# Wider value projection, other accumulator banks and more raw weight tiles in a hybrid attention block

## The chip, the cores and the metric

The kernel runs on one core of one Trainium2 chip. The metric is the device time of one execution in microseconds (us); lower is better. Before the change three runs gave 1017.72, 1018.07 and 1017.91 us, with a median of 1017.91 us. About 0.2% of that, 2 us, is what counts here as a difference.

## The reference

The kernel computes one layer of an encoder block for 512 positions and 1024 channels, in float32. Cut to what matters:

```python
h = x + 0.5 * rms_norm(swiglu_1(rms_norm(x)))
u = rms_norm(h)
q_a, k_a, v_a, q_b, k_b, v_b = split(u @ w_in)          # 6 x 512 columns, heads of 64
o_a = stick_breaking_attention(q_a, k_a, v_a)           # 8 heads, strictly causal
o_b = chunk_band_attention(q_b, k_b, v_b, rel_bias)     # 8 heads, own chunk and the 8 before
h = h + rms_norm(concat(rms_norm(o_a), rms_norm(o_b)) @ w_out)
h = h + 0.5 * rms_norm(swiglu_2(rms_norm(h)))
h = h + rms_norm((p @ w_ple) * sigmoid(h @ w_gate))
```

The change touches the first matrix products of `swiglu_1`, the last ones of it, the query and key product of heads 0 to 3 of the first group, and `v_a`, the values of the first group's eight heads.

## The kernel before, in words

**Operands.** Activations lie transposed: `h` holds 1024 channels as eight blocks k of 128 partitions by 512 positions. Every float32 operand is split in two float32r parts, a rounded `hi` and the rest `lo`, and every product is three matmuls (`mm3`, L235: hi by hi, lo by hi, hi by lo), so lines L236 to L238 of the profile hold nearly all of TensorE's work.

**Weights.** They arrive in chunks of 128 partitions by 1024 columns (512 KB). Each chunk is read by a DMA into a raw tile, then split (`split_to`, L305): ScalarE casts it to `wh` (L307) and VectorE subtracts that from the raw tile to give `wl` (L308). Raw tiles have tags: `wr` with two buffers, `wx` with three, `wy` with one. A DMA into a tag waits until the chunk that held the buffer has been split. The SyncE queue issues the DMAs in order, so one that waits for a buffer holds back those behind it. The first feed-forward part begins with eight plain chunks (wgu, numbers 0 to 7), all on `wr`; from chunk 8 on come the chunks of a fast matrix scheme that also uses `wx` and `wy`.

**Start.** A loop over j loads the eight blocks of `x` (L734, L737), the first chunks (L736) and the identity (L748). The first four products (`f_pl`, one per 128 output columns) go through k = 0 to 7, twelve matmuls for each k. The squares of `x` are summed block by block into `acc` (ScalarE squares into one buffer, L302; VectorE adds, L303). After 25 products TensorE needs this sum: `n_ss`, L250, eight small matmuls.

**End of the first feed-forward part and the joint.** `tail` computes the last six output blocks in two halves of 256 positions (tiles `f_dt`); VectorE adds each to `f` (L636) and to the sum of squares. The joint computes queries and keys of the first four heads (`pj`, four accumulators) for each half while the normalisation of that half is still being applied by VectorE (L358, L359, L311).

**Mixer.** The values of the first group follow (`values`, L840): for i = 0 (heads 0 to 3) and i = 1 (heads 4 to 7), for each block tb of 128 positions, eight products of 256 columns, then an evacuation by ScalarE and VectorE (L853, L854). A work list (`PLAN`) hands such products out: `fill(n)` runs n steps of it between the attention's own matmuls. After 15 steps the scores of head 0 begin: `scores` (L859) gives tile `z`, ScalarE makes two sigmoids of it (`fa`, L877, and `be`, L878), GpSimd masks them, VectorE scans (L883) and multiplies (L884), TensorE transposes (`pt`, L914).

**Accumulators.** PSUM has four tags, A, B, z and T, of two banks each. A new tile takes a bank of its tag and waits until the tile that held it has been read.

**Order.** TensorE's order is the order of the code. The other engines' order is made by a scheduler at build time; on the chip each engine runs its own list strictly in order.

Of the kernel before, what the change touches and what calls it, by code (L numbers as in the profile page):

```python
# [16 lines left out]
P = 128  # L17
# [34 lines left out]
TAIL_ROOT = 3  # L52
PLAN = (("v", 0, 0), ("v", 0, 1), ("qk", 2), ("qk", 3), ("v", 1, 0), ("qk", 4), ("qk", 5), ("qk", 6), ("v", 1, 1), ("qk", 7))

@with_exitstack
def block_kernel(ctx, tc, xT, pT, gains, ident_d, bias_d, wgu1, wst1, wd1, wdst1, wqk, wv, wo, wgu2, wst2, wd2, wdst2, wpp, wpg, gple, out):
    nc = tc.nc
# [68 lines left out]
    qk_chunks = [(wqk[g, i, j], 1024) for g in range(2) for i in range(4) for j in range(2)]  # L128
    v_chunks = [(wv[g, i, c], 1024) for g in range(2) for i in range(2) for c in range(2)]
    chunks.extend(qk_chunks[:4])  # L130
    for kind, *at in PLAN:
        if kind == "qk":
            chunks.extend(qk_chunks[2 * at[0]:2 * at[0] + 2])
        else:
            chunks.extend(v_chunks[4 * at[0] + 2 * at[1]:4 * at[0] + 2 * at[1] + 2])
    out_chunks = [(wo[g, c], 1024) for g in range(2) for c in range(4)]
# [19 lines left out]
    def emit_dma(cuts=1, queues=(nc.sync,)):  # L156
# [3 lines left out]
        if isinstance(n, tuple):  # L160
# [242 lines left out]
    def ffn(name, u, sp, pl, go, gpre, sa, sb, fa):  # L403
# [327 lines left out]
    for j in range(4):  # L731
# [36 lines left out]
    with tc.tile_pool(name="mx", bufs=1, reuse_waits="tile") as mp:  # L768
# [55 lines left out]
        def project(s):  # L824
            g, i = divmod(s, 4)
            pss = []
            for j in range(2):
# [10 lines left out]
                yield  # L838

        def values(g, i, tag):  # L840
            t = mp.tile([P, 4, 4, 2, 64], F32R, name=f"v{g}{i}", tag="v", bufs=3)
            vt[g, i] = t
            w = [get(), get()]
            for tb in range(4):
                pv = psum(tag, f"pv{g}{i}_{tb}", HT)
                for k in range(KD):
                    hi, lo = w[k // 4]
                    q = slice((k % 4) * HT, (k % 4 + 1) * HT)
                    mm3(pv[:], um[0][:, k, tb * P:(tb + 1) * P], um[1][:, k, tb * P:(tb + 1) * P],
                        hi[:, q], lo[:, q], k == 0, k == KD - 1)  # L850
                    if k == KD - 1:
                        src = pv.rearrange("p (h d) -> p h d", d=64)
                        act.activation(t[:, tb, :, 0, :], src, AF.Copy, scale=Rc[:, tb:tb + 1])  # L853
                        dve.scalar_tensor_tensor(t[:, tb, :, 1, :], src, Rc[:, tb:tb + 1],  # L854
                                                 t[:, tb, :, 0, :].bitcast(F32), ALU.mult, ALU.subtract)
                    if k % 2:
                        yield
# [160 lines left out]
        def work_list():  # L1018
            for n, (kind, *at) in enumerate(PLAN):
                yield from project(*at) if kind == "qk" else values(*at, "A" if n else "B")  # L1020
            mix_f.append(big("fm", 1, F32))
# [138 lines left out]

_ARGS = ["xT", "pT", "gains", "ident", "bias", "wgu1", "wst1", "wd1", "wdst1", "wqk", "wv", "wo", "wgu2", "wst2", "wd2", "wdst2", "wpp", "wpg", "gple"]

# [32 lines left out]
def _layout(i):  # L1195
# [10 lines left out]
    w_in = np.asarray(i["w_in"])[0]  # L1206
    qk, v = [], []
    for g in range(2):
        w = w_in[:, 1536 * g:1536 * g + 1024].reshape(KD, P, 2, 4, P)
        qk.append(w.transpose(3, 2, 1, 0, 4).reshape(4, 2, P, KD * P))  # L1210
        w = w_in[:, 1536 * g + 1024:1536 * (g + 1)].reshape(2, 4, P, 2, HT)
        v.append(w.transpose(3, 0, 2, 1, 4).reshape(2, 2, P, 4 * HT))
    a["wqk"] = np.stack(qk)
    a["wv"] = np.stack(v)
    w = np.asarray(i["w_out"])[0].reshape(2, 4, P, 4, 2, P)
# [25 lines left out]
```

## Time and profile before

| what | value |
|---|---|
| three runs, median | 1017.91 us |
| the profiled execution | 1017.77 us |
| its span | 1016.1 us |
| TensorE busy | 1001.5 us, 99% |
| weight loads busy | 944.4 us, 93% |
| VectorE, ScalarE, GpSimd busy | 780.8, 590.7, 133.7 us |
| granted TensorE clock | 0.998 |
| HBM read | 134.31 MB |

The span runs from the first to the last instruction on the core; the execution's own time is 1.7 us longer. A row of the timeline has the start, the duration, engine, line, operation, tile written and tiles read, and in brackets how long the engine was idle before and what ended that. Durations of matmuls overlap, so what a matmul costs is the distance from its start to the next start.

### The profile page before, as it was taken

Reading aid. Unit: us, or ns where it says so; the run is one execution under the profiler, and the core shown is the slowest. Engines: PE = TensorE matmul, PEld = TensorE weight load, DVE = VectorE, ACT = ScalarE, POOL = GpSimd, SP = SyncE. Lnnn points to the kernel's source line nnn. Section 1 sums busy time; section 2 is a strip of 40 time slices with the busy share of each in tenths; the row PEclk is TensorE's granted clock in tenths of the full one; section 3 lists DMA queues with packets and bytes.
Section 4 is the critical chain, followed back from the end, with each engine's and each line's share of the span. In section 5 each row is a group of like instructions: output and inputs, shape, how many; then the busy total and the mean of one; then the engine's idle time right before and its main releaser. Section 6 shows DMA issues by size and latency. Waiting matters only on the chain.

```text
span 1016.1 us, 18477 instructions
## 1 busy us (share of the span) xinstructions
PE 1001.5 (99%) x7242; PEld 944.4 (93%) x7242; DVE 780.8 (77%) x1370; ACT 590.7 (58%) x993; POOL 133.7 (13%) x221
## 2 busy tenths in 40 slices
PE   9999999999999999999999999999999999999997
PEld 7889999999999999888898799899999999999886
DVE  6777777677667888999999868786777677666856
ACT  6456554454456466777889655565543563455553
POOL 0001112112220003344000000011122112210000
PEclk9999999999999999999999999999999999999999
DMA  7338888979885213313323302268788888875102
GB/s 276 103 102 186 162 173 192 202 168 183 195 190 176 105 38 110 94 53 105 113 84 94 119 28 63 52 142 190 168 181 194 181 169 203 178 191 184 55 12 84
DMA packets 44855, 139.71 MB, mean 137 GB/s; under 512 B 5216, under 2 KB 5600, under 8 KB 44768
## 3 DMA queue, kind: packets, MB, share of 16 engines
q0 software_dynamic: 14976, 50.34, 30.6%
q1 hardware_dynamic: 28368, 85.83, 24.7%
q10 hardware_dynamic: 1424, 2.36, 0.9%
q8 instruction: 57, 0.93, 0.4%
q14 instruction: 30, 0.25, 0.1%
HBM read 134.31 MB, written 2.10 MB: 134 GB/s over the span
## 4 chain that ended last, share of the span: by engine, by line
PE 90%; DVE 5%; ACT 2%; DMA 1%; issue 1%; SPq 0%; POOL 0%; DVEq 0%; ACTq 0%; POOLq 0%
PE f_a L238 9%; PE f_a L236 9%; PE f_a L237 9%; PE f_c L236 4%; PE f_c L237 4%; PE f_c L238 4%; PE pj L236 3%; PE pj L237 3%; PE pj L238 3%; PE f_b L236 2%; PE f_b L237 2%; PE f_b L238 2%; PE f_d L238 2%; PE f_d L236 2%; PE f_d L237 2%; PE pt L914 2%
## 5 line engine op out<-in xcount | busy, mean ns | idle before, releaser
L308 DVE TENSOR_TENSOR wl<-wx,wh 128x1024 fp32r<-128x1024 f32 (+1 forms) x104 | 118.4, 1140 | 39.5 <-ACT wh L307 38.5
L307 ACT CAST wh<-wx 128x1024 fp32r<-128x1024 f32 (+1 forms) x104 | 101.6, 983 | 66.9 <-DMA wx<-in_wst_dram 38.9
L308 DVE TENSOR_TENSOR wl<-wr,wh 128x1024 fp32r<-128x1024 f32 (+2 forms) x100 | 109.4, 1100 | 27.2 <-ACT wh L307 26.1
L307 ACT CAST wh<-wr 128x1024 fp32r<-128x1024 f32 (+2 forms) x100 | 94.3, 950 | 43.2 <-DMA wr<-in_wgu_dram 11.1
L211 POOL DMA_DIRECT2D wx<-in_wst_dram x54 | 47.0, 870 | 413.3 <-DVE wl L308 349.7
L307 ACT CAST wh<-wy 128x1024 fp32r<-128x1024 f32 (+1 forms) x52 | 51.2, 985 | 41.8 <-DMA wy<-in_wdst_dram 15.7
L308 DVE TENSOR_TENSOR wl<-wy,wh 128x1024 fp32r<-128x1024 f32 (+1 forms) x52 | 59.2, 1139 | 11.0 <-ACT wh L307 10.8
L236 PE MATMUL pj<-um_hi,wh 128*128 128x512 f32 (+1 forms) x160 | 56.9, 355 | 1.1 <-DVE f_f L636 1.1
L237 PE MATMUL pj<-um_lo,wh 128*128 128x512 f32 (+1 forms) x160 | 55.9, 349 | 0.3 <-DVE um_lo L311 0.3
L238 PE MATMUL pj<-um_hi,wl 128*128 128x512 f32 (+1 forms) x160 | 55.8, 349 | 0.0
L238 PE MATMUL f_a<-f_U6h,wl 128*128 128x256 f32 x144 | 40.6, 282 | 0.0
L238 PE MATMUL f_a<-f_U3h,wl 128*128 128x256 f32 x144 | 40.5, 282 | 0.0
L237 PE MATMUL f_a<-f_U6l,wh 128*128 128x256 f32 x144 | 40.5, 282 | 0.0
L236 PE MATMUL f_b<-f_U1h,wh 128*128 128x256 f32 x144 | 40.5, 282 | 0.0
L237 PE MATMUL f_b<-f_U1l,wh 128*128 128x256 f32 x144 | 40.5, 282 | 0.0
L236 PE MATMUL f_c<-f_U4h,wh 128*128 128x256 f32 x144 | 40.5, 282 | 0.0
L237 PE MATMUL f_a<-f_U0l,wh 128*128 128x256 f32 x144 | 40.5, 281 | 0.0
L237 PE MATMUL f_a<-f_U5l,wh 128*128 128x256 f32 x144 | 40.5, 281 | 0.0
L236 PE MATMUL f_a<-f_U0h,wh 128*128 128x256 f32 x144 | 40.5, 281 | 0.0
L236 PE MATMUL f_a<-f_U5h,wh 128*128 128x256 f32 x144 | 40.5, 281 | 0.0
L236 PE MATMUL f_c<-f_U2h,wh 128*128 128x256 f32 x144 | 40.5, 281 | 0.0
L236 PE MATMUL f_a<-f_U6h,wh 128*128 128x256 f32 x144 | 40.5, 281 | 0.0
(476 smaller groups left out, 3883.5 us busy)
## 6 DMA issues: line engine op xcount, KB each, us to landing
wx<-in_wst_dram POOLq DMA_DIRECT2D x54, 512.0 KB, 5.6
wx<-in_wst_dram SPq DMA_DIRECT2D x18, 512.0 KB, 4.6
wy<-in_wst_dram SPq DMA_DIRECT2D x18, 512.0 KB, 6.1
wr<-in_wst_dram SPq DMA_DIRECT2D x18, 512.0 KB, 5.4
wy<-in_wst_dram POOLq DMA_DIRECT2D x18, 512.0 KB, 5.8
wx<-in_wdst_dram POOLq DMA_DIRECT2D x24, 384.0 KB, 4.8
wr<-in_wqk_dram SPq DMA_DIRECT2D x16, 512.0 KB, 3.7
wr<-in_wgu_dram SPq DMA_DIRECT2D x15, 512.0 KB, 4.4
```

Of the source, the lines that this page charges most:

```text
L211: pool.dma_start(out=r, in_=block, accum_op=ALU.add)
L236: pe.matmul(ps, hi, mh, start=start, stop=False, skip_group_check=skip)
L237: pe.matmul(ps, hi, ml, start=False, stop=False, skip_group_check=skip)
L238: pe.matmul(ps, lo, mh, start=False, stop=stop, skip_group_check=skip)
L307: a = act.copy(hi, src)
L308: b = dve.tensor_tensor(lo, src, hi.bitcast(F32), ALU.subtract)
L914: pe.transpose(pt[:, qi * P:(qi + 1) * P], aw[qi][:, (j - qi) * P:(j - qi + 1) * P], ident[:])
```

## The change

Three things are changed, and the order of the work follows from them.

1. **Values.** The first group's values are computed for all eight heads at once: per block tb eight products with 512 columns into one bank (`all_values`), instead of two passes with 256 columns. The weights are laid out for it in four chunks `wv0`, each with two k and 512 columns; all four chunks are wanted in the first block. Each block is evacuated in two pieces, one for each tile of four heads. The accumulators of the four blocks lie on tags z, z, B, B instead of B (i = 0) and A (i = 1). The joint's second norm is summed after 66 and spread after 72 products (`NMB`) instead of 68 and 81, since a product is now twice as wide.
2. **Banks.** The joint's four accumulators lie on A, A, B, B instead of A, A, z, z. The last six tiles of `tail` (second half) lie on A, z, A, z, z, z instead of z, A, z, A, z, A.
3. **Raw tiles.** Of the first eight chunks, numbers 0, 1, 2, 5, 6 and 7 use tag `wx`, 3 and 4 use `wr`: five raw buffers instead of two. Both halves of chunk 0 are issued on ScalarE's queue (before: one on ScalarE's, one on SyncE's). The identity is loaded after all of `x`.

```diff
-N1, Q1A, Q1B, NMA, NMB = (1, 25, 35), (13, 20), (8, 21), (34, 51), (68, 81)
+N1, Q1A, Q1B, NMA, NMB = (1, 25, 35), (13, 20), (8, 21), (34, 51), (66, 72)
-PLAN = (("v", 0, 0), ("v", 0, 1), ("qk", 2), ("qk", 3), ("v", 1, 0), ...
+PLAN = (("v", 0, 0), ("qk", 2), ("qk", 3), ("v", 1, 0), ...
...
-    v_chunks = [(wv[g, i, c], 1024) for g in range(2) for i in range(2) for c in range(2)]
+    v_chunks = [(wv0[c], 1024) for c in range(4)] + [(wv1[i, c], 1024) for i in range(2) for c in range(2)]
...
+    roomy = deep | set(range(2 * PLAIN))
...
-        tag = "wx" if i in deep and (i - (ple_at if i >= ple_at else mixer_at)) % 5 < 3 else "wr"
+        tag = "wx" if i in roomy and (i - max(x for x in (0, mixer_at, ple_at) if x <= i)) % 5 < 3 else "wr"
...
-                ps = psum("Az"[(m + hf) % 2], f"{name}_dt{m}_{hf}")
+                ps = psum("AzAzzz"[j] if hf else "Az"[m % 2], f"{name}_dt{m}_{hf}")
...
-            emit_dma(1 if j else 2, (nc.sync,) if j else (nc.scalar, nc.sync))
+            emit_dma(1 if j else 2, (nc.sync if j else nc.scalar,))
...
-        else:
-            nc.sync.dma_start(out=ident[:], in_=ident_d)
+    nc.sync.dma_start(out=ident[:], in_=ident_d)
...
-        pq = [psum("Az"[c // 2], f"pj00{c}") for c in range(4)]
+        pq = [psum("AB"[c // 2], f"pj00{c}") for c in range(4)]
...
+        def all_values():
+            ts, w = [v_tile(0, i) for i in range(2)], []
+            for tb in range(4):
+                pv = psum("zzBB"[tb], f"pv0_{tb}")
+                for k in range(KD):
+                    if len(w) <= k // 2:
+                        w.append(get())
+                    hi, lo = w[k // 2]
+                    q = slice(k % 2 * T, (k % 2 + 1) * T)
+                    mm3(pv[:], um[0][:, k, tb * P:(tb + 1) * P], um[1][:, k, tb * P:(tb + 1) * P],
+                        hi[:, q], lo[:, q], k == 0, k == KD - 1)
+                    if k == KD - 1:
+                        for i in range(2):
+                            v_out(ts[i], tb, pv[:, i * HT:(i + 1) * HT])
+                    yield
```

`v_out` holds the two evacuating instructions that stood in `values`; `v_tile` makes the tile. The second group's values stay as they were. One step of the work list is one product of 512 columns where it was two products of 256, so the first group's values still have 32 steps.

**VectorE at the start.** These rows stand on VectorE's list between the first feed-forward part's fifth square and the first small operation of its norm (`nx`); `wl3` to `wl6` are chunks 3 to 6. Before:

```order
L303 TENSOR_TENSOR acc_76<-acc_76,n1_4_sq_173 128x512
L303 TENSOR_TENSOR acc_76<-acc_76,n1_5_sq_176 128x512
L303 TENSOR_TENSOR acc_76<-acc_76,n1_6_sq_179 128x512
L303 TENSOR_TENSOR acc_76<-acc_76,n1_7_sq_182 128x512
L308 TENSOR_TENSOR wl3_151<-wr3_136,wh3_150 128x1024
L308 TENSOR_TENSOR wl4_209<-wr4_148,wh4_208 128x1024
L261 TENSOR_SCALAR nx_280<-n1_ss_275 128x4
```

Now:

```order
L304 TENSOR_TENSOR acc_76<-acc_76,n1_4_sq_173 128x512
L309 TENSOR_TENSOR wl4_209<-wr4_147,wh4_208 128x1024
L309 TENSOR_TENSOR wl5_239<-wr5_206,wh5_238 128x1024
L304 TENSOR_TENSOR acc_76<-acc_76,n1_5_sq_176 128x512
L304 TENSOR_TENSOR acc_76<-acc_76,n1_6_sq_179 128x512
L309 TENSOR_TENSOR wl6_269<-wr6_236,wh6_268 128x1024
L304 TENSOR_TENSOR acc_76<-acc_76,n1_7_sq_182 128x512
L262 TENSOR_SCALAR nx_280<-n1_ss_275 128x4
```

Before, all eight squares were added ahead of chunks 3 and 4. Now chunk 3 is split ahead of the fifth square (`wl3` stands five rows further up), and chunks 4, 5 and 6 stand ahead of the last addition. ScalarE's casts of these chunks have moved in the same way.

**ScalarE at the first scores.** The rows from the spread of the joint's second norm (`Rpre`) to the first sigmoids; `ks` are the keys of heads 0 to 3, cast from `qkf`. Before:

```order
L340 COPY Rpre_77<-nmb_rb_4395 128x256
L812 CAST ks000_4408<-qkf001_4418 64x512
L812 CAST ks100_4409<-qkf001_4418 64x512
L853 ACTIVATE v00_4291<-pv00_2_4391,Rc_79 128x4x64
L307 CAST wh123_4318<-wr123_4292 128x1024
L812 CAST ks001_4428<-qkf011_4438 64x512
L812 CAST ks101_4429<-qkf011_4438 64x512
L877 ACT_TABLE_LOAD
L877 ACTIVATE fa00_4490<-z000_4486,nRq_81 128x512
L878 ACTIVATE be00_4489<-z000_4486,Rq_80 128x512
```

Now:

```order
L341 COPY Rpre_77<-nmb_rb_4375 128x256
L846 ACTIVATE v01_4292<-pv0_0_4293,Rc_79 128x4x64
L812 CAST ks000_4388<-qkf001_4398 64x512
L812 CAST ks100_4389<-qkf001_4398 64x512
L812 CAST ks001_4408<-qkf011_4418 64x512
L812 CAST ks101_4409<-qkf011_4418 64x512
L900 ACT_TABLE_LOAD
L900 ACTIVATE fa00_4454<-z000_4450,nRq_81 128x512
L901 ACTIVATE be00_4453<-z000_4450,Rq_80 128x512
L846 ACTIVATE v00_4291<-pv0_1_4428,Rc_79 128x4x64
L900 ACTIVATE fa01_4480<-z001_4476,nRq_81 128x384
```

The cast of chunk 123 and one evacuation have left the place between the two pairs of keys; the table load still stands ahead of the first sigmoid.

**TensorE at the first two scores.** The rows ahead of the second score (`z001`), with the engines that each waits for. Before:

```order
L236 MATMUL pv01_0_4522<-wh121_4306,um_hi_3761 128x256
L237 MATMUL pv01_0_4522<-wl121_4307,um_hi_3761 128x256
L238 MATMUL pv01_0_4522<-wh121_4306,um_lo_3762 128x256
L864 MATMUL z001_4529<-ks000_4408,qd000_4404 128x384 [waits DVE_49]
L865 MATMUL z001_4529<-ks000_4408,ql000_4406 128x384
```

Now:

```order
L887 MATMUL z000_4450<-ks000_4388,qd000_4384 128x512 [waits DMAHW4_49,DVE_49,PE_49]
L888 MATMUL z000_4450<-ks000_4388,ql000_4386 128x512 [waits Pool_49]
L237 MATMUL pv0_1_4428<-wh122_4314,um_hi_3761 128x512
L238 MATMUL pv0_1_4428<-wl122_4315,um_hi_3761 128x512
L239 MATMUL pv0_1_4428<-wh122_4314,um_lo_3762 128x512
L237 MATMUL pv0_2_4472<-wh119_4296,um_hi_3761 128x512
L238 MATMUL pv0_2_4472<-wl119_4297,um_hi_3761 128x512
L239 MATMUL pv0_2_4472<-wh119_4296,um_lo_3762 128x512
L887 MATMUL z001_4476<-ks000_4388,qd000_4384 128x384 [waits Activation_49]
L888 MATMUL z001_4476<-ks000_4388,ql000_4386 128x384
```

Before, the second score took a bank that the joint's last accumulator had held and waited for VectorE's reading of that. Now the z tag's two banks hold the first two blocks of the values when the scores begin: the first three scores (`z000`, `z001`, `z002`) follow each other in the bank that `pv0_0` held, and `z003` takes that of `pv0_1`. So `z001` waits for the second sigmoid of `z000` on ScalarE.

More of the change, by code (lines that the diff above doesn't have):

```diff
@@ L134, in block_kernel @@
         else:
-            chunks.extend(v_chunks[4 * at[0] + 2 * at[1]:4 * at[0] + 2 * at[1] + 2])
+            chunks.extend(v_chunks[4 + 2 * at[1]:6 + 2 * at[1]] if at[0] else v_chunks[:4])
     out_chunks = [(wo[g, c], 1024) for g in range(2) for c in range(4)]
@@ L838, in project, with v_tile, v_out @@
                 yield
+        def v_tile(g, i):
+            vt[g, i] = mp.tile([P, 4, 4, 2, 64], F32R, name=f"v{g}{i}", tag="v", bufs=3)
+            return vt[g, i]
+        def v_out(t, tb, pv):
+            src = pv.rearrange("p (h d) -> p h d", d=64)
+            act.activation(t[:, tb, :, 0, :], src, AF.Copy, scale=Rc[:, tb:tb + 1])
+            dve.scalar_tensor_tensor(t[:, tb, :, 1, :], src, Rc[:, tb:tb + 1],
+                                     t[:, tb, :, 0, :].bitcast(F32), ALU.mult, ALU.subtract)
+        def all_values():
[13 more added lines that the diff above has]
+                    yield
         def values(g, i, tag):
-            t = mp.tile([P, 4, 4, 2, 64], F32R, name=f"v{g}{i}", tag="v", bufs=3)
-            vt[g, i] = t
+            t = v_tile(g, i)
             w = [get(), get()]
@@ L1019, in work_list @@
             for n, (kind, *at) in enumerate(PLAN):
-                yield from project(*at) if kind == "qk" else values(*at, "A" if n else "B")
+                yield from project(*at) if kind == "qk" else values(*at, "A") if n else all_values()
             mix_f.append(big("fm", 1, F32))
@@ L1158, in block_kernel @@
                 nc.sync.dma_start(out=out[tb * P:(tb + 1) * P, c0:c1], in_=e[:, tb, c0:c1])
[L1161 removed]
+_ARGS = ["xT", "pT", "gains", "ident", "bias", "wgu1", "wst1", "wd1", "wdst1", "wqk", "wv0", "wv1", "wo", "wgu2", "wst2", "wd2", "wdst2", "wpp", "wpg", "gple"]
 def _cols(g):
```

19 lines of the change are left out of this document (9 added, 10 removed).

## The prediction

> **What bounds the kernel now.** I read the page's first part, then TensorE's waits, then the timelines around them.
>
> ```profile
> PE 1001.5 (99%) x7242; PEld 944.4 (93%) x7242; DVE 780.8 (77%) x1370; ACT 590.7 (58%) x993; POOL 133.7 (13%) x221
> ```
>
> TensorE is busy for 99% of the span, so a change pays only by fewer or shorter steps of TensorE, or by a wait of TensorE taken away. Its waits (total, times, longest, in us), the two largest where the change works:
>
> ```profile
> PE pj L236 <- DVE f_f L636: 1.1, 1, 1.1
> PE pv L236 <- DVE v L854: 0.9, 1, 0.9
> ```
>
> Each is small beside 2 us, the least that counts as a difference. The question is how much of a wait really goes, and what comes in its place.
>
> **The change, part by part: width.** The values' 192 matmuls of 256 columns become 96 of 512. Steady stretches give the distance between starts: twelve rows of 256 columns, sixty-one of 512 columns at the start (the first after a wait), and two scores of 512 columns in the mixer.
>
> ```profile
> 377.67 0.28 PE L236 MATMUL pv<-wh,um_hi 128*128 128x256 f32 x1
> ...
> 378.99 0.28 PE L238 MATMUL pv<-wh,um_lo 128*128 128x256 f32 x1
> 9.52 0.50 PE L237 MATMUL f_pl<-u_lo,wh 128*128 128x512 f32 x1 [0.29 <-DVE u_lo L311]
> ...
> 23.26 0.39 PE L237 MATMUL f_pl<-u_lo,wh 128*128 128x512 f32 x1
> 389.35 0.39 PE L864 MATMUL z<-ks,qd 128*128 128x512 f32 x1
> 389.58 0.39 PE L865 MATMUL z<-ks,ql 128*128 128x512 f32 x1
> ```
>
> 256 columns: 1.32 / 11 = 0.120 us, 192 of them 23.0 us. 512 columns: 13.74 / 60 = 0.229, or 0.23; 96 of them 22.0 to 22.1. The width saves 0.9 to 1.1 us; I take 1.0. The Trainium skill (TensorE: Matmul & The Clock Gate, Back-to-back issue gap) has an isolated gap of N/2.4 + 2.5 ns; by it the estimate is 192 x 109.2 - 96 x 215.8 ns, a gain of 0.25 us only. The trace has 120 ns, not 109, at 256 columns, so the measured rows decide.
>
> **Start.** TensorE waits twice here: at 9.52 (row above) for block 1 of x, at 23.97 for chunk 3. In the chain of waits of this stretch the second half of chunk 0 stands first; then what all queues moved, and TensorE:
>
> ```profile
> 1.74 5.16 DMA wr<-in_wgu_dram
> 6.91 0.62 ACT wh L307
> GB/s 0 0 134 355 275 282 301 327 355 378 400 362 335 354 342 340 405 395 419 400 439 405 424 419 255 48 0 0 0 125 308 323 318 140 19 0 120 289 229 205
> 8.73 0.49 PE L236 MATMUL f_pl<-u_hi,wh 128*128 128x512 f32 x1
> 23.97 0.50 PE L238 MATMUL f_pl<-u_hi,wl 128*128 128x512 f32 x1 [0.33 <-DVE wl L308]
> 24.31 0.95 PE L250 MATMUL n_ss<-ones,acc 128*128 128x1 f32 x8
> ```
>
> And VectorE (x2 marks a row that stands for two in a run):
>
> ```profile
> 10.78 1.22 DVE L308 TENSOR_TENSOR wl<-wr,wh 128x1024 fp32r<-128x1024 f32 x1
> 17.58 0.69 DVE L303 TENSOR_TENSOR acc<-acc,n_sq 128x512 f32<-128x512 f32 x1
> 18.97 0.69 DVE L303 TENSOR_TENSOR acc<-acc,n_sq 128x512 f32<-128x512 f32 x1 [0.70 <-ACT n_sq L302]
> 20.36 0.69 DVE L303 TENSOR_TENSOR acc<-acc,n_sq 128x512 f32<-128x512 f32 x1 [0.70 <-ACT n_sq L302]
> 22.69 2.36 DVE L308 TENSOR_TENSOR wl<-wr,wh 128x1024 fp32r<-128x1024 f32 x2 [0.25 <-ACT wh L307]
> ```
>
> Chunk 3 now has a raw tile of its own, so its wait (23.97 - 23.26 - 0.23 = 0.5 us with the slow restart) goes. With both halves of chunk 0 on ScalarE's queue the second half no longer stands behind x; it lands earlier, u_lo of block 1 too, and the wait at 9.52 shrinks. But the first block of x now shares the DMA engines with that half: 256 KB at the 300 GB/s of the GB/s row are 0.85 us, so the first matmul is 0 to 0.85 later, I take half. The wait at block 1 costs 9.52 - 8.73 - 0.23, with the restart 0.7 us. Net I take 0.4 us gained (bounds 0 and 0.7). The Trainium skill (DMA: Bandwidth & Descriptors, Issuing engines are not separate DMA queues) says the same of the sharing: queues of all issuers interleave on the same 16 engines, so a queue adds no bandwidth.
>
> What comes in their place is the norm. `n_ss` needs the last square's addition, and TensorE would reach it at 24.31 - 0.5 - 0.4 = 23.4. VectorE's list now has chunk 3 ahead of the addition of the fifth square (17.58 before) and chunks 4, 5, 6 ahead of that of the eighth, the last. A split costs 2.36 / 2, less 0.04 of overlap, = 1.14 us; an addition that follows work directly 0.60 to 0.69. Chunk 1's split starts about 0.3 earlier, as the same bytes of x and chunks 0, 1 lie ahead of it on the DMA engines. So: the fifth square is added at 17.58 - 0.3 + 1.14 = 18.42; after it chunks 4 and 5, so the sixth is added at 18.42 + 0.6 + 2.28 = 21.30; the seventh one round with ScalarE later (20.36 - 18.97 = 1.39), 22.69. Chunk 6's cast stands behind the seventh square on ScalarE, so it begins about when that addition does, near 22.6; with this row's cast of 0.95 us
>
> ```profile
> L307 ACT CAST wh<-wr 128x1024 fp32r<-128x1024 f32 (+2 forms) x100 | 94.3, 950 | 43.2 <-DMA wr<-in_wgu_dram 11.1
> ```
>
> its split begins near 23.6 and ends at 24.75, and the last addition ends near 25.4. `n_ss` follows at about 25.4, 1.1 us later than now: TensorE would stand there for 2 us. The data is not what delays it: the GB/s row has slices of 0.85 us for the first 34 us; x, seven chunks, the first `wy` tile, identity and gains are 6.4 MB, which those slices reach at about 20 us, some 2 us ahead of the cast. I take +1.1 us for the start. Lower bound -0.9 (the additions in time), upper +1.5 (chunk 1 no earlier). VectorE's room afterwards, where chunks 5 and 6 were split so far, is worth nothing, since TensorE does not wait there.
>
> **Joint.** The bank wait of the second accumulator is real, but look at what follows it:
>
> ```profile
> 346.99 0.42 DVE L636 TENSOR_TENSOR f_f<-f_f,f_dt 128x256 f32<-128x256 f32 x1
> 348.50 0.28 PE L236 MATMUL f_dt<-f_sh,f_last5h 128*128 128x256 f32 x1
> 340.64 0.42 DVE L303 TENSOR_TENSOR acc<-acc,f_f_sq 128x256 f32<-128x256 f32 x1 [0.15 <-ACT f_f_sq L302]
> 341.12 0.61 PE L250 MATMUL q1a_ss<-ones,acc 128*128 128x1 f32 x4 [0.22 <-DVE acc L303]
> 352.28 0.39 PE L236 MATMUL pj<-um_hi,wh 128*128 128x256 f32 x1 [1.10 <-DVE f_f L636]
> 354.31 0.43 DVE L303 TENSOR_TENSOR acc<-acc,f_f_sq 128x256 f32<-128x256 f32 x1
> 354.89 0.58 PE L250 MATMUL q1b_ss<-ones,acc 128*128 128x1 f32 x4
> ```
>
> The wait costs 1.26 us with its restart. Eight products into the joint comes `q1b_ss`, which needs the sum that VectorE ends at 354.31. By the pair at 340.64 and 341.12 such a reader starts 0.48 after that addition starts: 354.79. VectorE's order here is unchanged and it runs without a gap, so TensorE, 1.2 us early, stands at `q1b_ss` until 354.8 instead. The joint gains 0.1 us (bounds 0 and 1.26); the wait goes from one place to the next. The new tags of `tail` cost nothing: the nearest case, its last tile, starts at 348.50 in a bank that VectorE has read by 346.99 + 0.42.
>
> **Mixer.** The wait at the values' third block (0.94 us idle, 1.2 with its restart) goes, because no bank is read late any more there. But the scores now share the z banks with the values, and the first three lie in one bank: `z001` waits until ScalarE has finished `be` of `z000`. When is that?
>
> ```profile
> 384.23 0.60 PE L294 MATMUL nmb_rb<-nmb_dg,ones 128*128 128x128 f32 x4
> 384.87 0.38 ACT L340 COPY Rpre<-nmb_rb 128x256 f32<-128x256 f32 x1 [0.33 <-PE nmb_rb L294]
> 388.49 0.68 DVE L809 TENSOR_TENSOR qkf<-pj,Rpre 128x512 f32<-128x512 f32 x1
> 389.78 1.26 ACT L812 CAST ks<-qkf 64x512 fp32r<-64x512 f32 x2
> 391.06 1.28 ACT L877 ACT_TABLE_LOAD   x1
> 392.35 0.69 ACT L877 ACTIVATE fa<-z,nRq 128x512 f32<-128x512 f32 x1
> 392.94 0.68 ACT L878 ACTIVATE be<-z,Rq 128x512 f32<-128x512 f32 x1
> 391.24 0.34 PE L864 MATMUL z<-ks,qd 128*128 128x384 f32 x1
> 398.26 0.39 PE L236 MATMUL pv<-wh,um_hi 128*128 128x256 f32 x1 [0.94 <-DVE v L854]
> ```
>
> In the clock of these rows: eight wide products after 377.67 and the norm's four small matmuls (0.36) put `nmb_rb` at 377.67 + 5.5 + 0.36, plus 0.1 for chunk 122's split, 383.65, 0.6 earlier. `Rpre` and `qkf` follow 0.6 earlier; one evacuation less stands between the two `qkf`, and chunk 123's cast no longer stands ahead of the second keys: second `qkf` 387.6, keys 388.3, table 389.6, `fa` 390.9, `be` done at 392.2. TensorE: `nmb_rb` 0.36, seven products of 0.686, `z000` 0.46, two products: 383.65 + 0.36 + 4.8 + 0.46 + 1.37 = 390.64. `z001` waits 1.5 us (bounds 0.5 and 2.5). `z002` comes four products (2.7 us) after `z001`, room enough for `fa` and `be` of that; `z003` three products later, when VectorE's second evacuation of `pv0_1` has had 5 us since `be` of `z000`. Together: -1.0 - 1.2 + 1.5 + 0.1 for chunk 122, that is -0.6 us (bounds -1.7 and +0.4).
>
> **Sum.** +1.1 - 0.1 - 0.6 = +0.4 us on a span of 1016.1. The profiled execution's own time, 1017.77, is 1.7 above its span and 0.14 below the runs' median, so the same sum on the median gives 1018.3 us: no measurable difference.
>
> **Rivals.**
>
> *The change does what it says.* All four waits go and nothing follows: 0.5 + 1.26 + 1.2 at three places, 1.0 by the width, 0.4 to 0.7 at block 1, some 4.5 us: 1013.4. For it: each wait is in the trace. Against: `q1b_ss` has only 0.1 us of room, and `z001` names ScalarE. Chance 0.09; half of it (about 1015.6) another 0.03.
>
> *The sum of squares is in time.* If ScalarE and VectorE get blocks 1 and 2 of x a microsecond sooner, `n_ss` is met at 23.4: start -0.9, total 1016.3. It decides below an `n_ss` of 24. Chance 0.18.
>
> *Chunk 6 lands late (slower).* In VectorE's new order, chunk 6's split stands ahead of the last addition. Beyond a landing of 22.6 us each microsecond delays `n_ss` by one. No pause between DMAs is left and the early `wy` tile stands ahead of it; at a landing of 25 the start costs 3.5, the total is 1020.7. Against: the GB/s row has its bytes moved by 20. Chance 0.07.
>
> *The width saves nothing.* If a wide matmul in the mixer starts 0.240 us after the one before, twice a narrow one, the term of 1.0 us is 0: 1019.3. Against: the two scores at 389.35 stand 0.23 apart. Chance 0.05. The isolated gap of the Trainium skill (TensorE: Matmul & The Clock Gate, Back-to-back issue gap) is nearest to this case.
>
> **How the numbers follow.** The forecast has 0.58. Faster by over 0.2% (below 1015.9) is 0.12, slower by over 0.2% 0.07, the rest, 0.81, no measurable change. The range reaches from half of the first rival to the forecast with all its upper bounds (+1.5, 0, +0.4): 1015.6 to 1019.8.
>
> **What would show it.** Right: TensorE's largest waits are `n_ss` for an addition (near 2 us), `q1b_ss` for an addition (near 1.1) and a score for `be` on ScalarE (near 1.5); the waits on `f_f` and `v` are gone; 512-column `pv` matmuls start 0.23 apart. Wrong: `n_ss` starting below 24.3, the joint's end earlier by a microsecond relative to the joint's start, or a score that does not wait. A new wait further on in the mixer, which I found no row for, would make the total wrong.

## The result, and the profile after

The change made the kernel slower: 1023.26 us, median of six runs, against 1017.99 before, ratio 1.0052 with a 95% interval of 1.0037 to 1.0067. The forecast was 1018.3 with a range up to 1019.8. The six runs lie between 1021.75 and 1026.77 us; the six of the kernel before lie between 1017.48 and 1018.22. So there are two things to explain: a loss of about 4 us in the best executions, and a spread of 5 us on top.

The profiled execution of the changed kernel took 1026.77 us, the longest of the six. Part 1 of its page and the row of the granted clock (40 slices of 25.6 us, tenths of full speed), and below them that row in the kernel before:

```profile
PE 1005.5 (98%) x7146; PEld 942.5 (92%) x7146; DVE 780.2 (76%) x1370; ACT 590.2 (58%) x993; POOL 133.0 (13%) x221
PEclk9899999999999999999999999999999999999999
```

```profile
PEclk9999999999999999999999999999999999999999
```

Matmuls fell by 96 as meant, yet busy time of TensorE rose by 4.0 us. Fewer instructions and more busy time means that some of them ran longer: the second slice has a clock of 8, where the kernel before has 9. Of TensorE's waits (total, times, longest, us), five that are new or much longer than before:

```profile
PE n_ss L251 <- DVE acc L304: 2.1, 1, 2.1
PE f_pl L237 <- ACT u_hi L311: 1.4, 1, 1.4
PE z L887 <- ACT be L901: 1.3, 1, 1.3
PE q1b_ss L251 <- DVE acc L304: 1.2, 1, 1.2
PE q2a_ss L251 <- DVE acc L304: 0.6, 1, 0.6
```

The waits that the change was to remove (`f_f`, `v`, `wl` of chunk 3) are gone. In their place stand the three that the prediction named, `n_ss`, `q1b_ss` and a score for `be`, and two that it did not name: 1.4 us before the very first product (it had that product 0 to 0.85 us later; here it is 1.09), and 0.6 at `q2a_ss`.

The windows of the start show what the waits do to the clock. Each row has the stretch, its length, the busy time and count of PE, PEld, DVE, ACT and POOL, the granted clock, the DMA share and GB/s:

```profile
4.20:7.60 3.40, 1.71 (x9) 1.14 (x8) 2.05 (x3) 2.63 (x5) 0.00 (x0) 1.00 1.03 367
7.60:11.00 3.40, 3.40 (x9) 2.67 (x8) 3.05 (x4) 3.40 (x7) 0.00 (x0) 0.50 1.03 407
11.00:24.70 13.70, 13.70 (x62) 11.27 (x61) 11.24 (x15) 8.63 (x13) 0.00 (x0) 1.00 0.91 343
24.70:28.10 3.40, 1.31 (x8) 0.81 (x6) 1.83 (x2) 1.58 (x2) 0.00 (x0) 1.00 0.03 12
28.10:31.50 3.40, 3.40 (x13) 3.01 (x13) 1.68 (x11) 0.00 (x0) 0.00 (x0) 0.50 0.49 154
31.50:34.90 3.40, 3.40 (x9) 2.63 (x9) 0.81 (x5) 0.69 (x2) 0.00 (x0) 0.50 0.00 0
```

Read the clock column against PE busy in the row before it. Where TensorE was busy for 1.71 or 1.31 us of 3.4, the next stretch is granted half the clock, once for 3.4 us and once for 6.8. In the kernel before, the clock is full from 5.7 us to 1012.6. The timeline around the second drop:

```profile
25.36 0.39 PE L239 MATMUL f_pl<-u_hi,wl 128*128 128x512 f32 x1
27.85 1.67 PE L251 MATMUL n_ss<-ones,acc 128*128 128x1 f32 x8 [2.09 <-DVE acc L304]
29.95 0.63 PE L238 MATMUL f_pl<-u_lo,wh 128*128 128x512 f32 x1
30.37 0.63 PE L239 MATMUL f_pl<-u_hi,wl 128*128 128x512 f32 x1
```

At full clock two 512-column products start 0.229 us apart; here it is 0.427, a price of 0.198 us each.

Where the 9.0 us of this execution (span 1025.1 against 1016.1) arise, read from when the same instruction starts in the two traces:

| instruction | before | after | later by |
|---|---|---|---|
| first `f_pl` | 5.18 | 6.26 | 1.09 |
| first `n_ss` | 24.31 | 27.85 | 3.54 |
| first `f_p` | 30.00 | 36.86 | 6.86 |
| first `f_dt` | 323.11 | 330.87 | 7.76 |
| first `pj` | 350.66 | 358.67 | 8.01 |
| first `pv` | 377.67 | 385.66 | 7.99 |
| last `po` | 564.56 | 572.65 | 8.09 |
| last `f_pl` of the second FFN | 628.00 | 636.08 | 8.08 |
| first `pe` | 948.66 | 957.67 | 9.02 |

The start has 6.9 of it; the joint gives nothing, the mixer +0.1. The steps of about 0.9 us, one within the first feed-forward part (FFN in the table) and one around `q2a_ss`, are taken up under the experiments.

### The profile page after: what moved, and what is told of

It is laid out like the page before. It is cut to its first block, busy times and chain, and to the rows that moved or that the text cites. A ratio compares the mean times of both kernels' runs of the same rounds, so it can differ in the third digit from the quotient of the medians.

```text
span 1025.1 us, 18293 instructions
## 1 busy us (share of the span) xinstructions
PE 1005.5 (98%) x7146; PEld 942.5 (92%) x7146; DVE 780.2 (76%) x1370; ACT 590.2 (58%) x993; POOL 133.0 (13%) x221
## 4 chain that ended last, share of the span: by engine, by line
PE 86%; DVE 8%; ACT 3%; DMA 1%; issue 1%; POOL 0%; DVEq 0%; SPq 0%; ACTq 0%; POOLq 0%
PE f_a L237 9%; PE f_a L239 9%; PE f_a L238 9%; PE f_c L237 4%; PE f_c L238 4%; PE f_c L239 4%; PE f_b L237 2%; PE f_b L238 2%; PE f_b L239 2%; PE pj L237 2%; PE pj L238 2%; PE pj L239 2%; PE f_d L239 2%; PE f_d L237 2%; PE f_d L238 2%; PE f_pl L237 2%
```

## Experiments

Twelve runs in three groups: eleven new kernels, and the change once more. Each group ran on a chip of its own, with its own runs of the kernel before: 1018.25 us in the first (23 runs, 1016.87 to 1019.9), 1018.38 in the second (30 runs), 1018.17 in the third (20 runs). Ratios are to these.

| run | what | median us | ratio, 95% interval |
|---|---|---|---|
| e1_rest_only | change without its start | 1019.49 | 1.0011 [1.0003, 1.0020] |
| e1_start_only | its start alone | 1023.47 | 1.0050 [1.0037, 1.0063] |
| e1_norm_later | norm's sum four products later | 1020.06 | 1.0011 [1.0002, 1.0019] |
| e1_more_warm | longer warm-up | 1022.89 | 1.0041 [1.0029, 1.0053] |
| e2_squares_first | squares ahead of chunks 4 to 6 | 1019.08 | 1.0009 [0.9999, 1.0019] |
| e2_squares_queues | and chunk 0 on two queues | 1017.74 | 0.9996 [0.9987, 1.0004] |
| e2_before_norm_early | before, norm's sum six products earlier | 1022.95 | 1.0038 [1.0023, 1.0052] |
| e2_values_ba | width alone, on free banks | 1017.33 | 0.9988 [0.9980, 0.9997] |
| e3_early_filled | e2_before_norm_early, its wait filled | 1020.93 | 1.0026 [1.0016, 1.0036] |
| e3_after_filled | change, wait at `n_ss` filled | 1021.96 | 1.0034 [1.0023, 1.0046] |
| e3_best | the good parts together | 1016.04 | 0.9978 [0.9970, 0.9987] |
| e3_after_again | the change unaltered | 1021.70 | 1.0039 [1.0023, 1.0054] |

The mean granted clock of an execution counts its stretches at half: one of 3.4 us in 1018 lowers it by 0.5 x 3.4 / 1018 = 0.0017. All 73 runs of the kernel before have 0.997 to 0.999. So 0.994 to 0.996 means one to two stretches more, and 0.993, in the profiled execution of the changed kernel, three. The mean has a gap: a trace's record of the clock begins with the first full grant, and what lies ahead of that counts as full. In the profiled execution of e3_after_again (mean 0.999) the record begins at 10.05 us, and these products ahead of it, 0.427 us apart, ran at half:

```profile
8.32 0.63 PE L238 MATMUL f_pl<-u_lo,wh 128*128 128x512 f32 x1
8.75 0.63 PE L239 MATMUL f_pl<-u_hi,wl 128*128 128x512 f32 x1
```

So the mean tells of drops after the first full grant, and not of a first grant that comes late.

### Which part carries the loss

e1_start_only, the kernel before with these lines:

```
-        tag = "wx" if i in deep and ... else "wr"
+        tag = "wx" if i in roomy and ... else "wr"
-            emit_dma(1 if j else 2, (nc.sync,) if j else (nc.scalar, nc.sync))
+            emit_dma(1 if j else 2, (nc.sync if j else nc.scalar,))
-        else:
-            nc.sync.dma_start(out=ident[:], in_=ident_d)
+    nc.sync.dma_start(out=ident[:], in_=ident_d)
```

> The kernel before with the first part of the change alone (both halves of chunk 0 on ScalarE's queue, five raw tiles for the first eight chunks, the identity last). Theory: the whole loss is here: n_ss waits 2.1 us, the clock is at half for 3.4 us or a multiple of it in some executions, 1021.7 to 1026.8 us with a median near 1023. Forecast's start term alone (+1.1): 1019.1. Rival (loss behind the start): below 1021.5, without half clock.

e1_rest_only, the changed kernel with the same lines turned back:

> The change without its first part: chunk 0's halves on two queues again, two raw tiles for the first weights, the identity loaded where it was. Width, values' banks, joint's banks and the norm's places stay. Theory (the loss is at the start: the wait for the first block of x, the wait at n_ss, and TensorE's clock at half after them): no half clock before 1010 us, n_ss without a wait, 1017.7 to 1018.3 us, as in the changed trace joint (-0.02) and mixer (+0.1) give nothing. Forecast's own terms for joint and mixer (-0.7): 1017.3. Rival (the loss is behind the start: 0.9 us in the first FFN and 0.9 at q2a_ss, which the changed trace shows): 1019.5 to 1020.

The start alone costs 5.2 us (1021.15 to 1025.54 in six runs, mean clocks from 0.994 to 0.999), as much as the whole change. The theory of this run held. In its profiled execution the sum waits as in the changed kernel:

```profile
27.46 1.05 PE L251 MATMUL n_ss<-ones,acc 128*128 128x1 f32 x8 [2.10 <-DVE acc L304]
```

The rest is not free, as I had expected it to be: 1019.49, where the rival had its number. But the trace puts only +0.55 us of it into the stretch from the first `pj` to the last `po`, and 0.37 of this is a longer wait for `um_lo` (0.71 against 0.34 us), which none of the other traces of the changed mixer has. What else is late there are the sums `q1a_ss` and `q2a_ss`, behind a cast that waits for a transfer. The cast ahead of `q2a_ss`, first in e1_rest_only, then in the kernel before:

```profile
936.81 1.05 ACT L307 CAST wh<-wr 128x1024 fp32r<-128x1024 f32 x1 [3.20 <-DMA wr<-in_wpg_dram]
```

```profile
934.95 1.05 ACT L307 CAST wh<-wr 128x1024 fp32r<-128x1024 f32 x1 [1.89 <-DMA wr<-in_wpg_dram]
```

Over all fourteen traces the wait at `q1a_ss` is between 0 and 0.9 us and that at `q2a_ss` likewise, in kernels whose work there is the same: 0.87 at `q1a_ss` in e3_early_filled, none in e2_squares_queues. It goes by the execution, and with 0.57 us idle at `q2a_ss` it is most of the 0.9 us up to `pe` in the profile of the change too. The 0.9 us within the first FFN there are two waits, the larger one 0.4 us at `f_c` for `f_f`; other executions have such a wait once, at other places (0.5 us in e2_squares_first, 0.8 in e3_after_filled) or not at all. How much of the 1.2 us of e1_rest_only is such chance was not settled; its interval begins at 0.3 us. The two parts, 5.2 and 1.2, add up to more than the 5.3 of the whole, which the widths of the intervals allow.

### Why the sum is late

The prediction had the last addition late because VectorE's list has splits ahead of it. The changed kernel's ScalarE, and VectorE behind it, say something else:

```profile
19.44 1.05 ACT L308 CAST wh<-wr 128x1024 fp32r<-128x1024 f32 x1 [2.03 <-PE f_pl L238]
22.39 0.63 ACT L303 ACTIVATE n_sq<-h 128x512 f32<-128x512 f32 x1 [1.37 <-DVE acc L304]
24.88 1.05 ACT L308 CAST wh<-wr 128x1024 fp32r<-128x1024 f32 x1 [1.86 <-PE f_pl L238]
25.84 0.62 ACT L303 ACTIVATE n_sq<-h 128x512 f32<-128x512 f32 x1
```

```profile
25.97 1.23 DVE L309 TENSOR_TENSOR wl<-wr,wh 128x1024 fp32r<-128x1024 f32 x1 [2.21 <-ACT wh L308]
27.11 0.68 DVE L304 TENSOR_TENSOR acc<-acc,n_sq 128x512 f32<-128x512 f32 x1
```

The casts wait for TensorE. `wh` and `wl` have four tiles each, so chunk 6 can be split only when TensorE has read the last of chunk 2. Its data was there: the last transfer of a `wgu` chunk in this stretch was issued at 13.6 us and none took over 7.6 us to land, so chunk 6 lay in its raw tile by 21.2, and the cast began at 24.88. On ScalarE the last square stands behind that cast, on VectorE the last addition behind that split. And `n_ss` stands one product behind the end of chunk 2. TensorE waits there for work that waits for TensorE, so the wait does not depend on when the start began: cast, split and addition, less the one product. It is 2.09 us in the changed kernel, 2.10 in e1_start_only, 2.10 in e1_more_warm and 2.10 in e3_after_again, though `n_ss` itself is reached at four different times. With the additions on a schedule of their own, as in the prediction, it would have shrunk by what TensorE came later.

e2_squares_first puts that to the test in the changed kernel:

```
-            with behind("evac"):
+            with behind("evac", *(("sq",) if 4 <= i < 7 else ())):
                 marks["split"] = split_to(hi[:, a:b], lo[:, a:b], r[:, a:b])
```

> The change with the casts of chunks 4, 5 and 6 put behind the norm's last square on ScalarE, as they stood before the change; raw tiles and queues stay as changed. Theory (the cast of chunk 6 waits for a split tile that TensorE frees only at the end of chunk 2, one product ahead of n_ss, and the last square stands behind that cast): n_ss no longer waits, no half clock near 28 us, only the late first product is left: 1018.8 to 1020.5 us, like the run with the norm's sum read later (1020.06). Rival of the forecast (VectorE's and ScalarE's own work makes the sum late, whatever TensorE does): n_ss still waits over a microsecond, 1022 or more.

ScalarE now has its last square, at 21.13, ahead of the casts of chunks 4 and 5, and of that of chunk 6, which again waits for TensorE:

```profile
21.13 0.63 ACT L303 ACTIVATE n_sq<-h 128x512 f32<-128x512 f32 x1 [0.76 <-DVE acc L304]
21.67 1.99 ACT L308 CAST wh<-wr 128x1024 fp32r<-128x1024 f32 x2
24.29 1.05 ACT L308 CAST wh<-wr 128x1024 fp32r<-128x1024 f32 x1 [0.63 <-PE f_pl L238]
```

`n_ss` starts without a wait, at 25.00, and the median falls to 1019.08. The theory held, and the rival that has VectorE's and ScalarE's own work make the sum late did not. e1_norm_later reads the sum later instead:

```
-N1, Q1A, Q1B, NMA, NMB = (1, 25, 35), ...
+N1, Q1A, Q1B, NMA, NMB = (1, 29, 39), ...
```

> The change with the norm's sum read after 29 products instead of 25 and spread after 39 instead of 35. Four products are 2.75 us, the wait was 2.1. Theory: the wait at n_ss goes, and with it the half clock at 28 to 35 us (3.1 us of matmuls); the wait for the first block of x and, in some executions, the half clock behind that stay: 1018.6 to 1020.5 us. Rival (what ends the start is the weights' split tiles, so the wait goes to a later place): 1022 us or more.

1020.06, also without a wait there and without a new one later in the start: its profiled execution, the shortest of its eleven, has the first `f_p` at 29.49, 0.5 us earlier than before the change. Both ways take the loss from 5 to between 0.7 and 1.8 us.

### Does a wait set the clock?

Three runs ask that. The first leaves the kernel before as it is but for one number, so that neither its transfers nor its queues change:

```
-N1, Q1A, Q1B, NMA, NMB = (1, 25, 35), ...
+N1, Q1A, Q1B, NMA, NMB = (1, 19, 35), ...
```

> The kernel before with its norm's sum read after 19 products instead of 25, nothing else. TensorE comes to n_ss near 20.2 us and the last addition ends at 22.4: a wait of 2.2 us and no other change. Theory (a wait of 2 us can put TensorE's clock at half for the next stretches): 2.2 less the wait for chunk 3 (0.5) is +1.7, and in part of the executions 1.5 to 3 us on top: median 1021 to 1023 us, widely spread, half clock within 25 to 33 us in some. Rival (the half clock belongs to the changed start, its transfers or queues): +1.7 alone, 1019.7 to 1020.2 us, no half clock.

Seven runs in two groups: 1020.17, 1020.67 and 1020.87 with a mean clock of 0.998, and 1022.95, 1023.11, 1024.11 and 1024.12 with 0.995 or 0.996. In the one group the loss is near what the wait lasts, and in the other 3 us more. No execution of the upper group has a trace, so its half clock is read from the mean alone. The profiled execution is of the lower group. Its sum waits even longer than in the changed kernel:

```profile
22.11 1.05 PE L250 MATMUL n_ss<-ones,acc 128*128 128x1 f32 x8 [2.70 <-DVE acc L303]
```

But the wait lies across two stretches, with TensorE busy for 1.61 and 2.49 us of them (windows as above):

```profile
17.80:21.20 3.40, 1.61 (x8) 0.99 (x6) 1.47 (x3) 1.76 (x3) 0.00 (x0) 1.00 0.79 324
21.20:24.60 3.40, 2.49 (x15) 2.23 (x16) 3.00 (x6) 2.01 (x3) 0.00 (x0) 1.00 0.08 16
24.60:28.00 3.40, 3.40 (x17) 2.80 (x16) 2.17 (x12) 0.92 (x1) 0.00 (x0) 1.00 0.85 263
```

The stretches are counted in 3.4 us from the clock's first full grant in that trace, at 4.1 us; the rounding of their ends moves a busy time by up to 0.1 us. e3_early_filled puts products of ones by ones, whose result is not used, where TensorE would stand:

```
         def sums():
+            if name == "n1":
+                stand = psum("T", "stand", P)
+                for _ in range(10):
+                    pe.matmul(stand[:], ones[:], ones[:], start=True, stop=True)
             chain(name, acc, c0, c1, D, Rc, root)
```

> The kernel before with its norm's sum read after 19 products, as in the run e2_before_norm_early, and ten products of ones by ones (20 passes of 0.107 us, 2.1 us) in front of that sum, so that TensorE works while it waits; their result is not used. Theory (the clock falls because TensorE stood still): the upper group of that run (1022.95 to 1024.12) is gone, all executions near its lower group, 1020.0 to 1021.0. Rival (the clock falls whatever TensorE does there, or the lost 3 us are something else): again two groups 3 us apart, median near 1022.9.

All nine runs have a mean clock of 0.997 to 0.999; none has the 0.995 or 0.996 that four of seven had, and the median is 2.0 us lower. The expectation of 1020 to 1021 was too narrow: the runs reach 1023.46, at 0.998. That longest one is the profiled execution, and its trace shows 1.6 us lost from the first `f_a` to `q1a_ss` (0.87 is the wait there) and 2.2 in the second FFN, all at full clock. The clock verdict rests on the clocks; the intervals of the two medians overlap.

e3_after_filled does the same with nine products in the changed kernel:

> The changed kernel with nine products of ones by ones (1.9 us) in front of the norm's sum, nothing else. Theory: the sum is as late as without them and the wait of 2.1 us is filled, the half clock near 28 us is gone; the one behind the first block of x stays in some executions: 1020.8 to 1022.5 us, median near 1021.3, against 1023.3 for the change. Rival (the clock is not set by the wait at n_ss): median 1023 or more, half clock near 28 us.

```profile
25.30 2.17 PE L340 MATMUL stand<-ones 128*128 128x128 f32 x18
27.64 1.02 PE L251 MATMUL n_ss<-ones,acc 128*128 128x1 f32 x8 [0.17 <-DVE acc L304]
```

The sum is as late as without them, no execution has less than 0.997, and the median is 1021.96. The unaltered change beside it, e3_after_again, came out at 1021.70, since this time four of its six runs had full clocks:

> The changed kernel unaltered, on the chip of the three runs above, for its spread. Theory (between none and three stretches of 3.4 us at half clock, 1.5 to 3 us each, by where the two waits fall): 1021 to 1027 us again, the longest with the lowest mean clock. Rival (the first executions were a chance): all within 1 us of each other.

Sorted, its times are 1019.84, 1021.40 and 1021.67 (all with a clock of 0.999), 1021.74 (0.998), 1023.62 (0.995) and 1025.45 (0.994). So the fill did not shorten the median on that chip. None of the five filled runs has the low clock of two of the six beside it, which on so few runs is a weak sign by itself; the nine of e3_early_filled carry more. The profiled execution of e3_after_again has the same wait of 2.10 us and no drop behind it, and so has that of e1_start_only, whose row stands below the two:

```profile
23.80:27.20 3.40, 1.65 (x8) 1.03 (x6) 1.53 (x2) 1.58 (x2) 0.00 (x0) 1.00 0.15 60
27.20:30.60 3.40, 3.05 (x17) 2.69 (x18) 1.97 (x12) 0.00 (x0) 0.00 (x0) 1.00 0.53 154
```

```profile
23.80:27.20 3.40, 1.56 (x7) 0.95 (x6) 1.62 (x2) 1.58 (x2) 0.00 (x0) 1.00 0.14 55
```

The execution of e3_after_again is 3.6 us longer than that of the kernel before, 3.35 of them by the first `f_p`. About 1.5 of this is the half clock up to 10.05 us: eight distances between starts take 3.40 us from 6.88 on, and 1.95 from 5.97 on in the kernel before.

The first stretch at half clock in the change's profile stands behind the wait before the first product. e1_more_warm fills that:

```
-WARM = 9
+WARM = 15
```

> The change with 15 warm-up products instead of 9: 12 more passes of 0.107 us fill the 1.4 us that TensorE stands before its first product. Theory (the clock follows how busy TensorE was in the stretch before): no half clock at 7.6 us, 1.6 us less in the executions that had it; the wait at n_ss and the half clock behind it stay: median 1021.5 to 1023. Rival (the half clock at 7.6 us has another cause than the wait): it stays, and the time is as changed or 0.1 longer.

It is gone (full clock from 6.3 to 26.7 us), and the other stays, behind a stretch in which TensorE was busy for 1.30 of 3.4 us:

```profile
23.30:26.70 3.40, 1.30 (x9) 0.81 (x7) 1.83 (x2) 1.58 (x2) 0.00 (x0) 1.00 0.25 96
26.70:30.10 3.40, 3.40 (x12) 2.92 (x13) 1.92 (x13) 0.00 (x0) 0.00 (x0) 0.50 0.47 147
30.10:33.60 3.50, 3.50 (x10) 2.73 (x9) 0.57 (x3) 0.69 (x2) 0.00 (x0) 0.51 0.00 0
```

The median, 1022.89, is as foretold and hardly below that of the change. Part of what the clock gives goes into the longer warm-up: `u_hi` is ready at 6.10 and the first product starts at 6.93, 0.67 us later than in the change's profile, while the stretch from there to `n_ss` is 2.2 us shorter. At the same place, around 6 to 10 us, five of the six traces with both halves of chunk 0 on one queue and nine warm-up products have TensorE at half clock. In the change's profile it fell there after a full grant at 4.2 us, in the other four the first full grant came as late as 9.6 to 10.2 us. e1_norm_later is the sixth: it waits 0.74 us before its first product and has the full clock from 6.1 us on. The kernels with two queues have it by 6.4 us. So the wait is not enough to bring this half clock, and that filling it takes it away rests on one trace.

### The queue of chunk 0

e2_squares_queues is e2_squares_first with

```
-            emit_dma(1 if j else 2, (nc.sync if j else nc.scalar,))
+            emit_dma(1 if j else 2, (nc.sync,) if j else (nc.scalar, nc.sync))
```

> As the run above, and the two halves of chunk 0 on two queues as before the change, so that of the first part only the five raw tiles and the identity's place are left. Theory (the half of chunk 0 on ScalarE's queue shares the DMA engines with the first block of x): first product back at 5.0 to 5.4 us, no wait before it, total 0.7 to 2 us below the run above: 1018.0 to 1019.5. Rival (the queue is not what delays the first product): first product at 5.9 us or later, the same total.

The activation that makes block 0 of `u_hi` waits for the first block of x. First e2_squares_first, then e2_squares_queues:

```profile
5.23 0.72 ACT L311 ACTIVATE u_hi<-h,gt 128x512 fp32r<-128x512 f32 x1 [1.04 <-DMA h<-in_xT_dram]
```

```profile
4.44 0.72 ACT L311 ACTIVATE u_hi<-h,gt 128x512 fp32r<-128x512 f32 x1
```

The first product starts at 6.00 in the one and 5.22 in the other, the first full grant of the clock comes at 9.6 and 5.9 us, and the median is 1.3 us lower, 1017.74, a little below the range of the theory and no longer distinguishable from the kernel before. So the second half on ScalarE's queue delays the first block of x by 0.8 us, where the prediction had taken half of that.

### The mixer

e2_values_ba keeps only the wider values (with the places of the norm that go with them), in banks that no score shares; start, `tail` and joint are turned back to before. The line of the banks, against the changed kernel:

```
-                pv = psum("zzBB"[tb], f"pv0_{tb}")
+                pv = psum("BBAA"[tb], f"pv0_{tb}")
```

> Only the width is left of the change: start and joint as before, and the 512-column values in the banks B, B, A, A, which the joint's products have left by then, so that no score shares a bank with them. Theory (width 0.74 by the changed trace, the wait on v of 1.2 gone, no wait of a score for be): 1.9 below before, 1016.0 to 1016.8 us. Rival (the third block waits for the first pair of joint's accumulators instead): 1017.3 or more, with a wait of pv on a read of pj.

The score that waits for ScalarE's `be` in the changed kernel, with what it follows, and the same pair of scores in e2_values_ba, without a wait:

```profile
398.68 0.39 PE L239 MATMUL pv<-wh,um_lo 128*128 128x512 f32 x1
400.36 0.44 PE L887 MATMUL z<-ks,qd 128*128 128x384 f32 x1 [1.30 <-ACT be L901]
```

```profile
389.13 0.39 PE L887 MATMUL z<-ks,qd 128*128 128x512 f32 x1
390.97 0.34 PE L887 MATMUL z<-ks,qd 128*128 128x384 f32 x1
```

1017.33 is 1.05 below the kernel before, less than the 1.9 expected: the theory missed. It is the rival's number, though not by its mechanism, as no `pv` waits for `pj`. In the traces the stretch from the first `pj` to the last `po` is 213.90 us before, 213.98 with the change, 212.55 in e2_values_ba. Added up start to start, the terms are: width -0.75 (192 distances of 0.1217 against 96 of 0.2356), the wait on `v` -1.1, and +0.45 by scores that now stand beside wide products and one more wait of `pt` for `tl`. Sharing the `z` banks adds 1.45 to that.

### The parts together

e3_best is e2_squares_queues with the values and the joint of e2_values_ba.

> What the runs so far left standing, put together: five raw tiles with the casts of chunks 4 to 6 behind the last square and chunk 0's halves on two queues (1017.74), and the 512-column values in the banks B, B, A, A with the joint as before (1.05 below before). Theory (the parts add up): 0.6 + 1.05 below before, 1016.3 to 1017.0 us. Rival (the parts cover the same waits): 1017.3 or more.

1016.04 us, ratio 0.9978 [0.9970, 0.9987]: 2.1 us below the kernel before and 5.7 below the changed kernel on the same chip. The parts add up, to a little more than the 1.65 us expected, and it is faster than both.

## Why the prediction was wrong

**The start's term, +1.1 us, is the step that failed**: it was +3.35 in the execution of e3_after_again, without a clock drop behind `n_ss`, and +6.9 in the profiled one. Three things in it were off.

- *The first product*: taken 0.4 later, bounds 0 and 0.85. It was 0.7 to 1.1 later in the six traces with the change's queue and nine warm-up products. The gain at block 1 of x was real, but a block that lies in front of everything was traded for it.
- *`n_ss`*: the forecast named this wait and its size, 2 us, and had the wrong reason. It was put down to VectorE's order of splits and additions, which would end at 25.4 whatever TensorE did; TensorE was to come at 23.4. What the traces show is a loop: square behind cast, cast behind a split tile, split tile behind TensorE. The wait has that size by itself, so whatever else delays the start is added to it in full. For the same reason the rival in which the sum of squares is in time (0.18) could not happen with the lists in this order. What I had not counted was the ring of four split tiles: five raw tiles let the scheduler put the casts of chunks 4 to 6 ahead of squares, but the split tiles that those casts write were still being read.
- *What a wait does afterwards*: nothing was set down for it. The half clock costs 1.6 us behind the first product (eight products by 0.198) and about 3 behind `n_ss` (twelve by 0.2, and 0.7 in the eight small ones). For the profiled execution the sum is 1.1 + 1.6 + 2.25 for `n_ss` with its restart + 3.1, less 0.56 and 0.49 for the two waits that went: 7.0, and 6.9 was read. For that of e3_after_again it is 0.9 + 1.5 + 2.25 less the same two: 3.6, and 3.35 was read. So even the mildest of the two has half clock at the start in it. That the forecast had 2 us of wait at `n_ss`, and 2.1 came, is luck: TensorE came 2 us later than it had reckoned, and the sum with it.

The Trainium skill has the rule that I left out (TensorE: Matmul & The Clock Gate, What's actually happening): TensorE's clock falls to half after at least one idle window of about 3.4 us, windows run on freely, and a busy one brings it back. The traces agree on the length (stretches of 3.4 and 6.8 us), on the half, and on the free run (the first full grant lies anywhere from 4.1 to 10.2 us), which fits that one kernel has executions with and without a drop behind the same wait. They do not agree on idle: 1.3 us busy of 3.4 was enough for a drop, and the longest gap was 2.1 us. Nor did one busy stretch bring the clock back behind `n_ss`: it took two, 6.8 us. The Trainium skill (the same page, HAM oscillation — how this bites in real kernels) warns of gaps above 3.4 us, by which nothing would have happened here.

**Joint, -0.1**: right. The wait on `f_f` went, `q1b_ss` waits 1.19 us instead (forecast 1.1), and in the milestones the joint gives nothing.

**Mixer, -0.6**: it was +0.1 to +0.3 in the traces without the chance wait for `um_lo`. The wait on `v` went (-1.1 against -1.2) and the score waits for `be` (1.45 with its restart against 1.5), both as worked out. Width gave 0.75 instead of 1.0, since the 512-column products stand 0.236 apart on the mean of the mixer and not 0.229 as in the start. The 0.45 by scores and `pt` was in no term.

**The rivals**: *the change does what it says* fell with its three new waits. *The width saves nothing* was wrong too: 0.75 us of the 1.0 came. *Chunk 6 lands late* came nearest: it had chunk 6's split ahead of the last addition as the place, but a transfer as the cause; chunk 6 was late by the split tile, not by its landing. The signs that would show the prediction right all came: the waits on the three named places, the two waits gone, and about 0.23 between `pv` products (0.236 on the mean). They tested the places, not the price of standing still at the start.

## What to carry to other kernels

When a load comes earlier, look for what its cast or copy will wait for next. If that is a tile that the consumer frees, everything queued behind the cast waits for the consumer as well, and it matters which work stands behind it. And a wait of TensorE is to be priced with what follows: in this kernel 2 us of standing still cost 2 us in some executions and 5 in others. Filling one with idle products took the drops away here, though no gain of the median was shown clear of the noise; taking the wait away was worth more.

## What was not expected of the hardware

TensorE's clock falls on less than a whole idle stretch. With 1.30 and 1.31 us busy of 3.4 the next stretches were granted half, twice in a row, although the first of the two was busy throughout; with 1.56, 1.61 and 1.65 they were not. At the start 1.71 us, part of it warm-up products of 128 columns, was followed by half clock as well, so the bound is not simply the busy time that the profile counts; it was not pinned down. How a wait falls into these stretches is a matter of the execution: of the thirty executions of the four kernels with a wait of 2 us or more at `n_ss` left unfilled, sixteen had a mean clock of 0.996 or less, against one of the 82 of the eight other kernels and none of the 73 of the kernel before. These means do not show a first full grant that comes late, and why that came only at 9.6 to 10.2 us in four traces stays open.
